# Stores of the gates and of the first Fourier half issued from ScalarE's queue, one tanh later, and another order in the last three iterations of a projection stage

## The chip, the cores and the metric

One core of a Trainium2 chip runs the whole kernel in one launch. The metric is the device time in microseconds (us); several executions are timed and the median counts. One further execution is taken by the hardware profiler. The engines are named as in the profile: PE (TensorE), PEld (its weight loads), DVE (VectorE), ACT (ScalarE), POOL (GpSimd), and SP (SyncE, which does no arithmetic and issues most of the transfers).

## The reference, cut to what matters

Two sequences of 2048 tokens with 1024 features each go through one layer with shared weights:

```python
u = _rmsnorm(h, g_norm)
z = u @ w_in
q, k, v, ga, f, gf = jnp.split(z, ...)
q = _apply_axial_rope(_rmsnorm(q, g_q), cos, sin)
k = _apply_axial_rope(_rmsnorm(k, g_k), cos, sin)
a = _blocked_gqa(q, k, v) * jax.nn.silu(ga)
fo = _fourier_branch(f, w_fmix) * jax.nn.silu(gf)
h = h + jnp.concatenate([a, fo], axis=-1) @ w_out
gate = jax.nn.sigmoid(_rmsnorm(h, g_ple) @ w_ple_gate)
return h + (p @ w_ple) * gate
```

A last RMSNorm follows. `_fourier_branch` is the real part of a 2-D DFT over positions and over the 64 channels of a group, and a linear map of each group. Here the names ga and gf are the columns of the projection that become the gate of the attention and the gate of the Fourier branch.

## The kernel before, in words

**Stages.** The first stage projects (function `project`, in the trace until about 759 us); the second does the attention, the second half of the Fourier branch, the output projection and the rest (until 2596 us). The change lies in the first stage and at the seam between the two.

**Chunks and iterations.** The 4096 tokens are cut into 16 chunks of 256 (two tiles of 128), the first 8 of one sequence and the next 8 of the other. `iteration(i)` (L868 to L927) is written for one chunk, n is 16, and three iterations follow the last chunk to finish it. In each the order of work on every engine is the order of the code: nothing is reordered by a scheduler. An iteration holds, in this order: loads; `square_z`; `lo_q(i-3)` (the second halves of split queries and keys: on DVE the rows named kd, ks, ksum, qs, L796 to L800, on SP the transposes qT and kT); `rope_q(i-2)` (DVE L767, POOL L772); `newton` (an inverse square root in some 20 small DVE steps, from `q_ss` L668 to `q_rs` L686); the matmuls of tile 0 for q, k and v (`mm_tile`); `norm_q` (POOL, qn and t); the folds; and the matmuls of tile 1.

**The sweep.** The other columns of a chunk (f, gf, ga) are a Python generator, the sweep of the chunk, which runs through the next iteration in pieces: `sweep_part(x)` advances it until about x us of matmuls were issued. Its pieces, in order: 24 pairs of matmuls for f (L1056, weights `w_f`, input `uf`; the result is copied by ACT into `ft`, L1024); two gf groups of 24 matmuls of 128x512 (`sweep_f`, through L1072); the first half of the Fourier transform, `first()`, two matmuls on `ft` (L1029) whose result ACT copies into `ge`; and four ga groups of 48 matmuls of 128x256 (`sweep_ga`, rows r = 0 to 3). After each gf and ga group `silu2` does a tanh on ACT (`th`, L1099) and a multiplication on DVE (`gt` or `gat`, L1101; for ga a maximum `tmax` follows, L1089).

**The stores.** Four results go to DRAM and come back in the second stage: `gfd` from `gt` (L1072, two in a chunk), `gd` from `ge` (L1038, one; in a sequence's first chunk two, L1041, and a small `gxd`, L1046), `agd` from `gat` (L1091, four). All are issued from POOL's queue, at the place of the code at which the piece of the sweep stands.

**The folds.** The input `uf` of the f matmuls is made from the chunk's `uc`: POOL adds (f_t L833) and forms sums (f_s L839), ACT rounds the high part (`uf`, L846), and DVE takes the remainder (`uf`, L847). This happens twice per chunk, with one f_s buffer pair: POOL's second f_s waits for DVE's first remainder. POOL's order in an iteration is f_t, f_s, f_t, then the stores that the sweep piece of 12.0 us issued, then the second f_s, then the other stores. ACT's second `uf` stands behind all tanhs of the chunk, and PE's next f group waits for both parts.

**Other work in between.** Every fifth sweep step advances a background generator that prepares the later weights (loads `w_st` on SP L390, conversions `w_o` on ACT L434 and DVE L435, stores wd on SP L437). Every fourth advances `self.ahead`, which takes the maxima of attention's first scores (two matmuls on PE, `a_mx` on DVE L1355).

**A shared ring.** ft, th, gt, ge, gat, w_st, w_o and a few others take turns in one ring of ten buffers (`nw2k = 10`, L181) of 2 KB per partition. A buffer that a store reads is free when the store has landed.

**The end of the stage.** In iterations 16, 17 and 18 `sweep_part(1000.0 if i < n else (6.0, 9.0, 5.0, 100.0)[i - n])` (L905) hands out the rest of the last sweep in portions. The transposes qT and kT of tiles 14 and 15 are issued there, and behind them on SP stands the load `bd` (L1204), for which the Fourier matmuls (L1173) at the head of the second stage wait. The last chunk's gates lie in buffers of their own (`g8`).

Of the kernel before, what the change touches and what calls it, by code (L numbers as in the profile page):

```python
# [48 lines left out]
EVEN = 8 * 33  # L49
# [116 lines left out]
class Build:  # L166
    def __init__(self, ctx, tc, a, y):
        self.ctx, self.tc, self.nc = ctx, tc, tc.nc
        self.a, self.y = a, y
        nc = self.nc  # L170
        ep = ctx.enter_context
        self.const = ep(tc.tile_pool(name="const", bufs=1))
        self.st = ep(tc.tile_pool(name="st", bufs=2))
        self.psF = ep(tc.tile_pool(name="psF", bufs=1, space=PSUM))
        self.psG = ep(tc.tile_pool(name="psG", bufs=2, space=PSUM))
        self.grouped, self.last_stores = False, nc.sync
        self.psX, self.nx = None, 0
        self.dq, self.d1, self.nflush, self.bg = None, [], 0, iter(())
        self.slow, self.passed, self.step = [], set(), 0
        self.ahead = iter(())  # L180
        self.nw2k = 10  # L181
        self.sc = {}
        d = lambda n, s, t: nc.dram_tensor(n, s, t, kind="Internal").ap()
        self.qTd = [d(f"qTd{s}", (NT, 128, 8, 128), F16) for s in range(2)]
        self.kTd = [d(f"kTd{s}", (2, 128, NT // 2, 3, 128), F16) for s in range(2)]
        self.vd = [d(f"vd{s}", (2, 128, NT, 64), F32) for s in range(2)]
        self.gd = [d(f"gd{s}", (128, NT // 2, 512), F32) for s in range(2)]
        self.gxd = [d(f"gxd{s}", (64, EVEN), F32) for s in range(2)]
        self.gfd = [d(f"gfd{s}", (NT, 128, 512), F32) for s in range(2)]
        self.fod = [d(f"fod{s}", (NT, 128, 512), F32) for s in range(2)]  # L190
        self.agd = [d(f"agd{s}", (2, 512, SEQ), F32) for s in range(2)]
        self.bdd = d("bdd", (128, 2, 512), F32)
        self.wd = {}
# [426 lines left out]
    def project(self, P, PU, W, early, later, wkv, wq, wf, wgf, wga, bg, mid):  # L620
# [3 lines left out]
        nc, st = self.nc, self.st  # L624
# [3 lines left out]
        n = len(steps)  # L628
# [239 lines left out]
        def iteration(i):  # L868
            nonlocal stores, stores_next
            if ok(i - 1) and i > 2:  # L870
                VL.pop((i - 1, 1))()
            if i == n + 3:
                self.last_stores = nc.gpsimd
            if ok(i + 4):
                load_x(i + 4, 0)
            if ok(i - 1):
                load_rope(i - 1)
            stores, stores_next = stores_next, []
            for f in stores:
                f()  # L880
            del stores[:]
            sq = square_z(i - 1) if ok(i - 1) else None
            if ok(i - 3):
                lo_q(i - 3)
            if ok(i - 2):
                rope_q(i - 2)
            rs = None
            if ok(i - 1) or ok(i + 2):
                rs = newton(i - 1 if ok(i - 1) else None, i + 2 if ok(i + 2) else None, sq)
            if ok(i):  # L890
                mm_tile(i, 0)
            if ok(i):
                sweep_part(4.0)
                VL.pop((i, 0))()
                sweep_part(4.0)
            if ok(i - 1):
                norm_q(i - 1, rs)
            if folds(i):
                fold_u(i, 0)
                fold_s(i, 0)  # L900
                fold_u(i, 1)
                sweep_part(12.0)
                fold_hl(i, 0)
                fold_s(i, 1)
            sweep_part(1000.0 if i < n else (6.0, 9.0, 5.0, 100.0)[i - n])  # L905
            if folds(i):
                fold_hl(i, 1)
            if ok(i + 2):
                hi_u(i + 2)
                for tt in range(CH):  # L910
                    lo_u(i + 2, tt)
            if ok(i + 4):
                load_x(i + 4, 1)
            if ok(i - 2):
                hi_q(i - 2)
            if ok(i):
                mm_tile(i, 1)
                append(i)
            if ok(i + 3):
                sq_u(i + 3)  # L920
            if i == n - 3:
                early()
            if i == n:
                later()
            if i == n + 3:
                self.drain(bg)
                self.drain(self.ahead)  # L927
# [86 lines left out]
    def sweep_f(self, s, c, uc, UF, i, pool, W):  # L1014

        nc = self.nc
        CH = 2
        w2k = lambda n, k=512: pool.tile([128, 512], F32, name=n, tag="w2k", bufs=self.nw2k)
        F = []
        half = (slice(0, EVEN), slice(EVEN, 512))  # L1020

        def out(ps):
            F.append(w2k("ft"))
            nc.scalar.activation(F[-1][:], ps[:], AF.Copy, scale=self.sc["inv_f"][:])  # L1024

        def first():
            pf = self.bank()
            if c:
                nc.tensor.matmul(pf[:], self.dft1[:], F[0][:], start=True, stop=True)  # L1029
            else:  # L1030
                for y, sl in enumerate(half):
                    for t in range(CH):
                        nc.tensor.matmul(pf[64 * t:64 * t + 64, sl], self.dft1x[:, 2 * t + y], F[t][:, sl],
                                         start=True, stop=True)
            ge = w2k("ge")
            nc.scalar.activation(ge[:], pf[:], AF.Copy)
            if c:
                nc.gpsimd.dma_start(self.gd[s][:, c, :], ge[:])  # L1038
                return 0.86
            for t in range(CH):  # L1040
                nc.gpsimd.dma_start(self.gd[s].rearrange("(g y i) t d -> y g i t d", g=8, y=2)[t, :, :, 0, :],  # L1041
                                    ge[64 * t:64 * t + 64])
            px, gx = self.bank(), w2k("ge")
            nc.tensor.matmul(px[0:64, :EVEN], self.dft1x[:, 4], F[0][:, :EVEN], start=True, stop=True)
            nc.scalar.activation(gx[0:64, :EVEN], px[0:64, :EVEN], AF.Copy)
            nc.gpsimd.dma_start(self.gxd[s], gx[0:64, :EVEN])  # L1046
            return 1.3

        if c:
            ps = self.bank()  # L1050
            uf = UF.pop(i)
            n = 0
            for k in range(8):
                for ia, ib in SPLIT3:
                    for y, sl in enumerate(half):
                        nc.tensor.matmul(ps[:, sl], uf[:, y, ia, k, :], W["f"][:, ib, k, sl], start=n == y == 0,  # L1056
                                         stop=n == 23, skip_group_check=True)
                    n += 1
                yield 0.64
            out(ps)  # L1060
        else:
            for tt in range(CH):
                ps = self.bank()
                yield from self.mm(ps[:], lambda b, k: uc[:, tt, b, k, :], lambda b, k: W["f"][:, b, k, :])
                out(ps)
        for tt in range(CH):
            t = c * CH + tt
            ps = self.bank()
            yield from self.mm(ps[:], lambda b, k: uc[:, tt, b, k, :], lambda b, k: W["gf"][:, b, k, :])
            gt = w2k("gt")  # L1070
            self.silu2(gt[:], ps[:], self.sc["h_gf"], w2k("th"),
                       lambda t=t, gt=gt: nc.gpsimd.dma_start(self.gfd[s][t], gt[:]))  # L1072
        yield first()

    def sweep_ga(self, s, c, uc, pool, W):

        nc = self.nc
# [4 lines left out]
        for r in range(4):  # L1082
            ps = self.bank()
            yield from self.mm(ps[:, :n], lambda b, k: W["ga"][:, b, k, r * 128:(r + 1) * 128],
                               lambda b, k: uc[:, :, b, k, :], n)
            gt, th = (w2k("gat")[:, :n], w2k("th")) if g8 is None else (g8[:, 2 * r], g8[:, 2 * r + 1])

            def more(r=r, gt=gt):
                nc.vector.tensor_reduce(out=self.tmax[s][:, c * 4 + r:c * 4 + r + 1], in_=gt, op=ALU.max,  # L1089
                                        axis=AX.X, apply_absolute_value=True)  # L1090
                nc.gpsimd.dma_start(self.agd[s][1, r * 128:(r + 1) * 128, c * n:(c + 1) * n], gt)  # L1091

            self.silu2(gt, ps[:, :n], self.sc["h_ga"], th, more)

    def silu2(self, out, z, half, th, then):

        nc = self.nc
        n = out.shape[-1]
        nc.scalar.activation(th[:, :n], z, AF.Tanh, scale=half[:])  # L1099

        self.defer(lambda: nc.vector.scalar_tensor_tensor(out=out, in0=th[:, :n], scalar=1.0, in1=z,  # L1101
                                                          op0=ALU.add, op1=ALU.mult), True)
# [941 lines left out]
```

## Time and profile before

| | us |
|---|---|
| median of three executions | 2601.84 |
| the three executions | 2595.85, 2603.52, 2601.84 |
| the profiled execution's own time | 2597.87 |
| its span, first to last instruction | 2595.8 |
| PE busy in the span | 2511.0 |
| POOL busy | 1896.6 |
| DVE busy | 1668.4 |
| ACT busy | 1183.6 |

The 2.1 us between the profiled execution's time and its span lie before the first and behind the last instruction. In the timeline a row gives start and duration of a run of like instructions, engine, line, operation, output<-input, count, and in brackets the engine's idle time before it with what ended that. A row of SP is marked SPq: the engine issues a transfer there, and the duration is that of the issue.

### The profile page before, as it was taken

How to read it: one execution, taken by the hardware profiler on the slowest of the kernel's cores; microseconds unless marked ns; L12 is line 12 of the kernel's file. 1: busy time of each engine (PE TensorE's matmuls, PEld its weight loads, DVE VectorE, ACT ScalarE, POOL GpSimd, SP SyncE). 2: the span in 40 equal slices, each digit the busy share in tenths (PEclk: the TensorE clock that was granted, in tenths of full speed). 3: DMA queues.
4: the chain of work that ended last, by engine and by line, in shares of the span. 5: the costliest groups of instructions: out<-in, count | busy, mean ns of one | idle time of the engine just before them, and what ended most of it. 6: DMA issues, size and time to landing. Idle time of an engine off the chain costs nothing. (4 is left out here: it accounts for less than half of the span.)

```text
span 2595.8 us, 49879 instructions
## 1 busy us (share of the span) xinstructions
PE 2511.0 (97%) x19896; PEld 1384.0 (53%) x19896; DVE 1668.4 (64%) x2382; ACT 1183.6 (46%) x1983; POOL 1896.6 (73%) x1646
## 2 busy tenths in 40 slices
PE   6999989999999999999999999999999999999988
PEld 3566656666656545545545555445544554545533
DVE  7766576777566856566666666666666665766534
ACT  4433353434235545554544545444544444445522
POOL 0465545475659978888888888878887988888840
PEclk9999999999999999999999999999999999999999
DMA  8467588787377742223222233422223322233232
GB/s 259 101 175 198 162 223 230 185 195 180 103 197 248 212 118 62 58 76 78 59 69 75 71 81 88 90 69 63 73 73 82 72 75 63 66 82 76 78 76 53
DMA packets 450265, 297.92 MB, mean 115 GB/s; under 512 B 294000, under 2 KB 394480, under 8 KB 450032
## 3 DMA queue, kind: packets, MB, share of 16 engines
q1 hardware_dynamic: 437952, 256.28, 38.9%
q0 software_dynamic: 12080, 38.46, 4.2%
q8 instruction: 155, 2.54, 0.4%
q14 instruction: 78, 0.64, 0.1%
HBM read 146.12 MB, written 82.45 MB: 88 GB/s over the span
## 5 line engine op out<-in xcount | busy, mean ns | idle before, releaser
L1325 POOL TENSOR_TENSOR acc<-acc,p 128x1024 f32<-128x1024 f32 x384 | 927.6, 2416 | 109.5 <-ACT p L1320 84.6
L1320 ACT ACTIVATE p<-ps_s,s_scale 128x512 f32<-128x512 f32 x1024 | 648.1, 684 | 636.4 <-PE ps_s L1317 613.9
L1355 DVE TENSOR_REDUCE a_mx<-ps_m 128x1 f32<-128x1024 f32 x498 | 608.9, 1223 | 512.0 <-PE ps_m L1347 501.0
L1649 PE MATMUL ps_g<-w_pg,hT 64*128 64x512 f16 x2784 | 494.1, 376 | 3.8 <-DVE seen L1610 2.4
L1383 PE MATMUL ps_o<-p,v 128*64 128x256 f32 x4096 | 468.2, 381 | 0.0
L1317 PE MATMUL ps_s<-q,k 64*128 64x512 f16 x3072 | 433.1, 378 | 1.4 <-ACT p L1320 1.0
L1383 PEld LDWEIGHTS ps_o<-p,v 128*64 128x64 f32 x4096 | 283.7, 137 | 160.4 <-issue 28.5
L504 PEld LDWEIGHTS <-uc 128*128 128x128 f16 x2400 | 236.3, 99 | 231.2 <-DMA uc<-hl 19.5
L1649 PEld LDWEIGHTS <-hT 64*128 64x128 f16 x2784 | 204.8, 94 | 156.9 <-issue 15.7
L1649 PE MATMUL ps_g<-w_wo,mh 64*128 64x512 f16 x1440 | 260.5, 376 | 3.2 <-DVE mh L1554 1.9
L1649 PE MATMUL ps_g<-w_wo,mT 64*128 64x512 f16 x1440 | 257.3, 376 | 0.0
L1317 PEld LDWEIGHTS <-k 64*128 64x128 f16 x3072 | 152.6, 94 | 195.3 <-issue 77.0
L1347 PE MATMUL ps_m<-k,q 64*128 64x512 f16 x996 | 200.8, 377 | 10.2 <-DVE a_mx L1355 9.8
L504 PEld LDWEIGHTS <-w_ga 128*128 128x128 f16 x1536 | 148.8, 98 | 33.5 <-issue 11.9
L1323 POOL TENSOR_TENSOR acc<-p,p 128x1024 f32<-128x1024 f32 x64 | 150.8, 2357 | 11.7 <-ACT p L1320 10.7
L1649 PEld LDWEIGHTS <-mh 64*128 64x128 f16 x1440 | 101.5, 94 | 91.5 <-issue 16.6
L1649 PEld LDWEIGHTS <-mT 64*128 64x128 f16 x1440 | 107.0, 94 | 76.3 <-issue 4.8
L772 POOL TENSOR_TENSOR t<-t,t 128x640 f32<-128x640 f32 x32 | 49.2, 1556 | 121.2 <-DVE t L767 121.2
L1406 DVE RECIPROCAL ps_f<-ps_f 128x256 f32<-128x256 f32 x61 | 107.1, 1756 | 13.6 <-PE ps_f L1399 13.6
L504 PE MATMUL ps_x<-uc,w_ga 128*128 128x256 f16 x1008 | 113.5, 273 | 2.0 <-DVE a_mx L1355 1.4
L504 PE MATMUL ps_x<-w_gf,uc 128*128 128x512 f16 x480 | 108.0, 384 | 2.4 <-DVE a_mx L1355 2.4
L1390 ACT ACTIVATE at<-ps_o,a_scale 128x256 f32<-128x256 f32 x64 | 30.4, 474 | 168.2 <-PE ps_o L1383 168.2
(347 smaller groups left out, 3415.6 us busy)
## 6 DMA issues: line engine op xcount, KB each, us to landing
q<-qTd SPq DMA_DIRECT2D x256, 64.0 KB, 2.2
ag<-agd SPq DMA_DIRECT2D x64, 256.0 KB, 3.5
out<-h POOLq DMA_DIRECT2D x31, 512.0 KB, 3.1
x<-in_x_prompt SPq DMA_DIRECT2D x16, 512.0 KB, 4.9
gfd<-gt POOLq DMA_DIRECT2D x32, 256.0 KB, 2.7
agd<-gat POOLq DMA_DIRECT2D x64, 128.0 KB, 2.8
w_st<-in_w_out SPq DMA_DIRECT2D x32, 256.0 KB, 4.0
w_st<-in_w_ple_gate SPq DMA_DIRECT2D x32, 256.0 KB, 4.0
```

Of the source, the lines that this page charges most:

```text
L504: self.nc.tensor.matmul(ps, lhs(ia, k), rhs(ib, k), start=(i == 0), stop=(i == 3 * ks - 1))
L772: nc.gpsimd.tensor_tensor(out=t1[:, tt], in0=t1[:, tt], in1=t2[:, tt], op=ALU.add)
L1317: nc.tensor.matmul(S[u][e][:], w[sl], q[sl].rearrange("p h q -> p (h q)"), start=j == i == 0, stop=i + 1 == len(todo), skip_group_check=True)
L1320: nc.scalar.activation(p[:, e, :], S[u][e][:], AF.Exp, scale=self.sc["s_scale"][:])
L1323: nc.gpsimd.tensor_tensor(out=ACC[u][:], in0=P[u, 0][:], in1=p[:], op=ALU.add)
L1325: nc.gpsimd.tensor_tensor(out=ACC[u][:], in0=ACC[u][:], in1=p[:], op=ALU.add)
L1347: nc.tensor.matmul(ps[c], Q[u][0][sl, h, :], kt[s, kv, half][sl, :, 0, :], start=True, stop=True)
L1355: nc.vector.reduce_max(MX[u][:, h, half, c:c + 1], x, axis=AX.X)
L1383: nc.tensor.matmul(o[64 * f:64 * f + 64], vt[s, kv, c // 8][:, c % 8, :], p[:, e, f], start=(c == 0), stop=(c == 15))
L1390: nc.scalar.activation(at[:].rearrange("p c q -> p (c q)"), o, AF.Copy, scale=self.sc["a_scale"][:])
L1406: nc.vector.reciprocal(r, r)
L1649: nc.tensor.matmul(g[0][:], g[1](ia, k)[sl], g[2](ib, k)[sl], start=a, stop=z, skip_group_check=True)
```

## The change: what it does

1. The stores gfd, gd, gxd and agd are no longer issued where their results are made. They are put in a list (`self.stores`), and `store_gates()` issues the list's content from ACT's queue. It is called right behind each tanh, and behind the copy `ft`. A result is made by DVE after its tanh, so its store stands behind the next tanh (or the next `ft`).
2. The last chunk's four agd stores (from `g8`) stay on POOL.
3. In iteration 16 a `sweep_part(7.2)` is put ahead of `newton`, in iteration 17 a `sweep_part(3.9)` ahead of `lo_q`, and the table of the portions becomes (3.3, 3.3, 7.0, 100.0).

```diff
+            if i == n + 1:
+                sweep_part(3.9)
             if ok(i - 3):
                 lo_q(i - 3)
             if ok(i - 2):
                 rope_q(i - 2)
             rs = None
+            if i == n:
+                sweep_part(7.2)
             if ok(i - 1) or ok(i + 2):
                 rs = newton(i - 1 if ok(i - 1) else None, i + 2 if ok(i + 2) else None, sq)
...
-            sweep_part(1000.0 if i < n else (6.0, 9.0, 5.0, 100.0)[i - n])
+            sweep_part(1000.0 if i < n else (3.3, 3.3, 7.0, 100.0)[i - n])
...
         def out(ps):
             F.append(w2k("ft"))
             nc.scalar.activation(F[-1][:], ps[:], AF.Copy, scale=self.sc["inv_f"][:])
+            self.store_gates()
...
-                nc.gpsimd.dma_start(self.gd[s][:, c, :], ge[:])
+                self.stores.append((self.gd[s][:, c, :], ge[:]))
...
-                       lambda t=t, gt=gt: nc.gpsimd.dma_start(self.gfd[s][t], gt[:]))
+                       lambda t=t, gt=gt: self.stores.append((self.gfd[s][t], gt[:])))
...
-                nc.gpsimd.dma_start(self.agd[s][1, r * 128:(r + 1) * 128, c * n:(c + 1) * n], gt)
+                d = self.agd[s][1, r * 128:(r + 1) * 128, c * n:(c + 1) * n]
+                if g8 is None:
+                    self.stores.append((d, gt))
+                else:
+                    nc.gpsimd.dma_start(d, gt)
...
+    def store_gates(self):
+        for d, x in self.stores:
+            self.nc.scalar.dma_start(d, x)
+        del self.stores[:]
...
         nc.scalar.activation(th[:, :n], z, AF.Tanh, scale=half[:])
+        self.store_gates()
```

The order of PE's instructions and of SP's is the same before and after. Three places show what moves on the others.

ACT, in the middle of the first stage, from a chunk's second gf tanh (h_gf) to its second `uf`; first before:

```order
L1099 ACTIVATE th<-ps_x,h_gf 128x512
L1036 ACTIVATE ge<-ps_x 128x512
L434 ACTIVATE w_o<-w_st,wf_s 128x512
L1099 ACTIVATE th<-ps_g,h_ga 128x256
L434 ACTIVATE w_o<-w_st,wf_s 128x512 x2
L846 ACTIVATE uf<-f_s 128x2x512
L1099 ACTIVATE th<-ps_g,h_ga 128x256
L434 ACTIVATE w_o<-w_st,wf_s 128x512 x2
L1099 ACTIVATE th<-ps_f,h_ga 128x256
L434 ACTIVATE w_o<-w_st,wf_s 128x512
L1099 ACTIVATE th<-ps_x,h_ga 128x256
L846 ACTIVATE uf<-f_s 128x2x512
```

and the first rows of the same stretch after the change:

```order
L1114 ACTIVATE th<-ps_x,h_gf 128x512
L1107 DMA gfd<-gt 128x512
L1042 ACTIVATE ge<-ps_x 128x512
L435 ACTIVATE w_o<-w_st,wf_s 128x512
L1114 ACTIVATE th<-ps_g,h_ga 128x256
L1107 DMA gfd<-gt 128x512
L1107 DMA gd<-ge 128x512
L435 ACTIVATE w_o<-w_st,wf_s 128x512 x2
L847 ACTIVATE uf<-f_s 128x2x512
L1114 ACTIVATE th<-ps_g,h_ga 128x256
L1107 DMA agd<-gat 128x256
L435 ACTIVATE w_o<-w_st,wf_s 128x512 x2
```

Each tanh is now followed by the store of the result before it: two more agd stores stand in the cut-off rest, one behind each of the two tanhs there, and the fourth agd of a chunk stands behind the next chunk's `ft`.

POOL, the folds of one chunk in the same stage, before:

```order
L833 TENSOR_TENSOR f_t<-uc 128x512 x2
L839 TENSOR_TENSOR f_s<-f_t 128x512 x2
L833 TENSOR_TENSOR f_t<-uc 128x512 x2
L1072 DMA gfd<-gt 128x512 x2
L1038 DMA gd<-ge 128x512
L1091 DMA agd<-gat 128x256
L839 TENSOR_TENSOR f_s<-f_t 128x512 x2
L1091 DMA agd<-gat 128x256 x3
```

After the change the four rows of stores are gone from here, and the four rows of folds stand behind one another.

DVE, at the seam, from the last step of `newton` of tile 15 (q_rs) to the start of the last `lo_q` (the second kd row; t is the rotation of tile 15, and a number in a name only tells buffers apart); first before:

```order
L686 TENSOR_SCALAR q_rs<-rsq_z_8406,inv_kv 128x2x2
L1355 TENSOR_REDUCE a_mx<-ps_x 128x1 x2
L796 TENSOR_TENSOR kd<-kd,ks 128x256
L797 CAST ks<-kd 128x2x2x64
L798 TENSOR_TENSOR kd<-kd,ks 128x256
L799 TENSOR_TENSOR ksum<-t_8062,kd 128x256
L800 TENSOR_TENSOR qs<-t_8062,qs 128x16x64
L767 TENSOR_TENSOR t_8528<-qn,rt 128x16x16 x4
L767 TENSOR_TENSOR t_8528<-qn,rt 128x4x16 x4
L1355 TENSOR_REDUCE a_mx<-ps_x 128x1 x2
L1101 SCALAR_TENSOR_TENSOR gt<-th,ps_x 128x512 x2
L796 TENSOR_TENSOR kd<-kd,ks 128x256
```

and after the change:

```order
L687 TENSOR_SCALAR q_rs<-rsq_z_8480,inv_kv 128x2x2
L1117 SCALAR_TENSOR_TENSOR gt<-th,ps_x 128x512 x2
L797 TENSOR_TENSOR kd<-kd,ks 128x256
L798 CAST ks<-kd 128x2x2x64
L799 TENSOR_TENSOR kd<-kd,ks 128x256
L800 TENSOR_TENSOR ksum<-t_8062,kd 128x256
L801 TENSOR_TENSOR qs<-t_8062,qs 128x16x64
L768 TENSOR_TENSOR t_8586<-qn,rt 128x16x16 x4
L768 TENSOR_TENSOR t_8586<-qn,rt 128x4x16 x4
L1117 SCALAR_TENSOR_TENSOR gat_8599<-gat_8599,ps_x 128x256
L1095 TENSOR_REDUCE tmax_88<-gat_8599 128x1
L797 TENSOR_TENSOR kd<-kd,ks 128x256
```

The two pairs of maxima a_mx are gone from here: all four now stand ahead of `newton`. The two gf products gt stood behind the rotation of tile 15 and now stand ahead of the `lo_q` of tile 14. The first ga product and its maximum stood behind the last `lo_q` and now stand ahead of it.

More of the change, by code (lines that the diff above doesn't have):

```diff
@@ L181, in __init__ @@
         self.nw2k = 10
+        self.stores = []
         self.sc = {}
@@ L1037, in first @@
             if c:
-                nc.gpsimd.dma_start(self.gd[s][:, c, :], ge[:])
+                self.stores.append((self.gd[s][:, c, :], ge[:]))
                 return 0.86
             for t in range(CH):
-                nc.gpsimd.dma_start(self.gd[s].rearrange("(g y i) t d -> y g i t d", g=8, y=2)[t, :, :, 0, :],
-                                    ge[64 * t:64 * t + 64])
+                self.stores.append((self.gd[s].rearrange("(g y i) t d -> y g i t d", g=8, y=2)[t, :, :, 0, :],
+                                    ge[64 * t:64 * t + 64]))
             px, gx = self.bank(), w2k("ge")
@@ L1045, in first @@
             nc.scalar.activation(gx[0:64, :EVEN], px[0:64, :EVEN], AF.Copy)
-            nc.gpsimd.dma_start(self.gxd[s], gx[0:64, :EVEN])
+            self.stores.append((self.gxd[s], gx[0:64, :EVEN]))
             return 1.3
```

## The prediction

> **What bounds the kernel now.** I read the busy row first, then the releasers of PE's waits in the first stage, then PE's clock by stretches.
>
> ```profile
> span 2595.8 us, 49879 instructions
> PE 2511.0 (97%) x19896; PEld 1384.0 (53%) x19896; DVE 1668.4 (64%) x2382; ACT 1183.6 (46%) x1983; POOL 1896.6 (73%) x1646
> ```
>
> PE works 2511.0 of 2595.8 us. The change doesn't touch PE's order, so it can only return what PE loses waiting, 84.8 us in all, and in the part of the program that it edits. PE's waits between 90 and 760 us name that part (total, times, longest):
>
> ```profile
> PE ps_g L1056 <- ACT uf L846: 5.1, 2, 3.6
> PE ps_x L504 <- DVE a_mx L1355: 3.8, 2, 2.4
> PE ps_x L1056 <- ACT uf L846: 2.1, 2, 1.5
> PE ps_x L1056 <- DVE uf L847: 1.9, 2, 1.1
> PE ps_g L1056 <- DVE uf L847: 1.3, 2, 0.7
> ```
>
> The four uf rows sum to 10.4 us: f groups that wait for the fold's result, four chunks in all. The a_mx row, 3.8 us, is the seam. The next view says what the clock adds (columns: stretch, its length, busy time with count of PE, PEld, DVE, ACT, POOL, granted clock, DMA share, GB/s):
>
> ```profile
> 325.00:390.00 65.00, 58.51 (x379) 38.30 (x377) 47.00 (x85) 35.57 (x61) 30.21 (x31) 0.95 0.83 224
> 455.00:520.00 65.00, 65.00 (x443) 43.36 (x442) 47.55 (x123) 30.80 (x59) 31.43 (x36) 1.00 0.77 186
> ```
>
> Where PE waits, the granted clock is 0.95; where it doesn't, PE is busy for all 65 us at 1.00, and there the change can give nothing. Now PE at the four chunks, which I call C, D, E and F:
>
> ```profile
> 153.79 0.61 PE L1056 MATMUL ps_x<-w_f,uf 128*128 128x264 f16 x4 [0.63 <-ACT uf L846]
> 155.49 2.36 PE L1056 MATMUL ps_x<-w_f,uf 128*128 128x264 f16 x20 [1.09 <-DVE uf L847]
> ...
> 284.34 0.61 PE L1056 MATMUL ps_g<-w_f,uf 128*128 128x264 f16 x4 [1.50 <-ACT uf L846]
> 285.60 3.89 PE L1056 MATMUL ps_g<-w_f,uf 128*128 128x264 f16 x20 [0.65 <-DVE uf L847]
> ...
> 330.88 0.61 PE L1056 MATMUL ps_x<-w_f,uf 128*128 128x264 f16 x4 [1.46 <-ACT uf L846]
> 332.27 3.64 PE L1056 MATMUL ps_x<-w_f,uf 128*128 128x264 f16 x20 [0.79 <-DVE uf L847]
> ...
> 379.82 0.61 PE L1056 MATMUL ps_g<-w_f,uf 128*128 128x264 f16 x4 [3.60 <-ACT uf L846]
> 381.08 3.94 PE L1056 MATMUL ps_g<-w_f,uf 128*128 128x264 f16 x20 [0.65 <-DVE uf L847]
> ```
>
> The same twenty matmuls take 2.36 us at C, and 3.89, 3.64 and 3.94 behind the longer waits: 1.53, 1.28 and 1.58 us more. So each longer wait costs its idle time and about 1.5 us of slower matmuls. At stake: C 0.63+1.09 = 1.7, D 1.50+0.65+1.53 = 3.7, E 1.46+0.79+1.28 = 3.5, F 3.60+0.65+1.58 = 5.8; together 14.7 us.
>
> The Trainium skill ("TensorE: Matmul & The Clock Gate", "What's actually happening") puts the half clock down to at least one idle window of about 3.4 us. By that D and E would not have been slowed and would return 2.2 us each; the rows show 1.3 to 1.5 us of slowing behind idle times of 2.2 us in two pieces, and the sum goes by the rows.
>
> **The change part by part: the stores.** Does a store make uf late? F shows it most plainly (POOL, SP and ACT by time):
>
> ```profile
> 362.29 1.11 POOL L1072 DMA_DIRECT2D gfd<-gt  x2
> ...
> 372.06 2.94 POOL L839 TENSOR_TENSOR f_s<-f_t 128x512 f32<-128x512 f32 x2 [7.59 <-DVE uf L847]
> ...
> 364.68 0.34 SPq L390 DMA_DIRECT2D w_st<-in_w_out  x1
> 365.11 0.53 SPq L437 DMA_DIRECT2D wd_wp<-w_o  x1
> ...
> 368.98 0.72 ACT L434 ACTIVATE w_o<-w_st,wf_s 128x512 f16<-128x512 f32 x1 [4.17 <-DMA w_st<-in_w_out]
> ...
> 378.34 0.47 ACT L1099 ACTIVATE th<-ps_x,h_ga 128x256 f32<-128x256 f32 x1 [2.88 <-DMA agd<-gat]
> 378.71 1.05 ACT L846 ACTIVATE uf<-f_s 128x1024 f16<-128x1024 f32 x1
> ```
>
> It is a ring of causes. POOL issues the two gfd behind three fold steps, at 362.29. A w_st load wants a buffer of the shared ring, and SP's queue stands until 364.68. ACT's w_o waits 4.17 us for a load, and ACT's first uf stands behind it, so POOL's second f_s waits 7.59 us. At last ACT waits 2.88 us for an agd store before the tanh ahead of the second uf, and PE waits 3.60 for that uf. After the change no store stands on POOL between folds, and none waits for a fold. I take F at 5.0 of 5.8 (bounds 0 and 5.8), since a store still stands one tanh late. At C both waits (1.7) have the same source and I take them whole; the lower bound is 0. D has a direct cause:
>
> ```profile
> 271.29 0.74 POOL L1072 DMA_DIRECT2D gfd<-gt  x1
> 272.05 0.54 POOL L1038 DMA_DIRECT2D gd<-ge  x1
> 272.58 0.54 POOL L1091 DMA_DIRECT2D agd<-gat  x1
> 280.72 2.48 POOL L839 TENSOR_TENSOR f_s<-f_t 128x512 f32<-128x512 f32 x2 [7.60 <-issue]
> ```
>
> Three stores, 0.74+0.54+0.54 = 1.8 us, stand ahead of the f_s that ends last. Without them uf is 1.8 us sooner: the wait of 1.50 closes, 0.3 of the 0.65 stays, and the slow matmuls go: 3.4. The 7.60 us of POOL's own issue stay. E I take at 2.3, between 0 and 3.5, nearer to the upper end because F, with the same conversions in its chunk, is its nearest row.
>
> **The price on ACT.** Seven issues a chunk. SP's rows above bound one between 0.34 and 0.53 us, POOL's at 0.54; I take 0.5, so 3.5 us a chunk, or 4 to 5 in the stretch of 65 us in which ACT is busy 35.57. ACT's spare time there, 29 us, hides it; without that cover the tanh behind it, and then the uf, would be late by 0.5 a store. ACT also waits at each store for DVE's product, made from the previous tanh; it is long done by the next one, which follows a matmul group later (2.7 us or more). Ahead of the second uf stands one store, 0.5, which F's reserve covers.
>
> **The seam.** The order of PE, DVE, POOL and SP there:
>
> ```profile
> 731.52 5.34 PE L504 MATMUL ps_x<-w_gf,uc 128*128 128x512 f16 x24
> 739.28 7.03 PE L504 MATMUL ps_x<-w_gf,uc 128*128 128x512 f16 x24 [2.42 <-DVE a_mx L1355]
> 748.52 5.40 PE L504 MATMUL ps_x<-uc,w_ga 128*128 128x256 f16 x48 [1.36 <-DVE a_mx L1355]
> 765.46 1.10 PE L1173 MATMUL ps_g<-bd,fT 128*128 128x256 f32 x4 [2.16 <-DMA bd<-bdd]
> ...
> 738.54 1.28 DVE L1355 TENSOR_REDUCE a_mx<-ps_x 128x1 f32<-128x512 f32 x2
> 739.74 0.51 DVE L796 TENSOR_TENSOR kd<-kd,ks 128x256 f32<-128x256 f32 x1
> 745.65 2.22 DVE L767 TENSOR_TENSOR t<-qn,rt 128x256 f32<-128x256 f32 x8
> 748.99 1.27 DVE L1101 SCALAR_TENSOR_TENSOR gt<-th,ps_x 128x512 f32<-128x512 f32 x2
> 752.80 0.42 DVE L796 TENSOR_TENSOR kd<-kd,ks 128x256 f32<-128x256 f32 x1 [2.54 <-ACT ks L786]
> ...
> 748.03 3.04 POOL L772 TENSOR_TENSOR t<-t,t 128x640 f32<-128x640 f32 x2 [1.99 <-DVE t L767]
> ...
> 755.70 2.61 SPq L804 DMA_TRANSPOSE qT<-qs  x2
> 760.37 1.31 SPq L1204 DMA_DIRECT2D bd<-bdd  x1
> ```
>
> With the four a_mx ahead of newton PE's second gf group starts at 736.86 and takes 5.34, not 7.03: it is done at 742.2 instead of 746.3, and with the 1.36 PE reaches attention 5.5 us sooner. But the Fourier matmuls of 765.46 wait for bd, whose load stands on SP behind the transposes, which stand behind the last lo_q, POOL's t, DVE's rotation and tile 14's lo_q, at 739.74. That lo_q now stands behind both gt, and the second needs the tanh of the gf group done at 742.2. With 0.7 of tanh and 0.64 of gt the lo_q begins at 743.5, 3.8 us later. (The four a_mx, 2.56 by 1.28 for two, also push newton, which ended at 738.54, to 741.1; that is ahead of 743.5 and adds nothing.) Some returns: a_mx and gt no longer stand behind the rotation, and the lo_q that took 5.9 us (739.74 to 745.65) took under 2.9 the second time (752.80 to 755.70). So bd comes 0.65 (of a gat and its maximum ahead of the last lo_q) to 3.8 us later; I take +2.5. Then PE's sooner start turns into a longer wait for bd. The other end, with bd no bound, is −5.5.
>
> **Sum.** C 1.7 + D 3.4 + E 2.3 + F 5.0 = 12.4 us less, seam 2.5 more: −9.9. From the profiled execution's own 2597.87 that gives 2588.0. It lies 4.0 under the median of the runs, 2601.84, and these spread from 2595.85 to 2603.52, so for the median I forecast 2590.
>
> **Rivals.**
> - *The seam gains too.* If the transposes wait for less than I think, PE keeps the 5.5: 2597.87 − 12.4 − 5.5 = 2580. For it: the lo_q's 5.9 against 2.9 us. Against: PE already waited 2.16 for bd.
> - *The change doesn't do what it says.* Each store stands a tanh later, the fourth agd of a chunk even behind the next ft, so buffers of the ring come free no sooner and w_st, th and uf wait as before: gaps stay, seam +2.5, 2600. For it: ACT already waits at a tanh for agd (2.88). Against: F's store waited for a fold, and D's stores were direct work of POOL.
> - *Slower: ACT stalls at a store.* The transposes hold SP's issue 1.3 us each (2.61 for two). If a store on ACT cannot be issued meanwhile, the second uf behind it comes 1.3+0.5 = 1.8 us late, in up to 14 chunks. It decides where uf has less than 1.8 us to spare; at four chunks it had none. With half the chunks hit, no gap closed and the seam's +2.5: 2597.87 + 7 × 1.8 + 2.5 = 2613. For it: the second uf stands straight behind a store. Against: beside F's stores SP issues plain transfers of 0.34 and 0.53. The Trainium skill ("Perfetto Trace Analysis", "DMA Instruction — HWDGE") says that transfers of this kind lock one shared descriptor generator for the time of their issue, which is this mechanism; no run here shows it yet, as only SP issued so.
>
> **How the numbers follow.** Chances: forecast 0.50 (its own range 2582 to 2597, from E and F at their bounds), seam gains too 0.15, stores don't help 0.25, ACT stalls 0.10. Two in ten outside: the range is 2578 to 2603, which leaves out the stall and the tails. A measurement tells about 0.3% from no change, 7.8 us, so faster means below 2594: four fifths of the forecast and all of the seam's gain, 0.55; slower is the stall, 0.10; same is the rest, 0.35.
>
> **What would show it.** Right: no uf waits of PE at C, D and F and a clock of 1.00 from 260 to 390; POOL's second f_s straight behind its f_t; no releaser gfd on SP's loads; PE's wait for bd grown to some 8 us or more, with the first attention scores sooner. Wrong: uf waits of the same size with agd still named ahead of the tanh; SP's or ACT's issues far above 0.54 us; the bd load no later than 760.37 less what was gained before it.

## The result, and the profile after

| | before | after |
|---|---|---|
| median, us | 2601.62 | 2586.09 |
| lowest to highest (4 executions each) | 2595.85 to 2603.52 | 2585.38 to 2587.85 |
| the profiled execution, us | 2597.87 | 2585.38 |
| its span, us | 2595.8 | 2583.6 |

The ratio is 0.9945 (95% interval 0.9933 to 0.9957): 15.5 us less in the median. The median before in this table has one execution more than the one that the forecast started from.

First PE's waits between 90 and 760 us in the changed kernel (total, times, longest; the line numbers are those of the changed kernel, 1 to 16 higher), all six of them:

```profile
PE ps_g L1189 <- DMA bd<-bdd: 5.8, 1, 5.8
PE ps_g L1243 <- DVE gat L1117: 3.4, 1, 3.4
PE ps_x L505 <- DMA uc<-hl: 1.2, 1, 1.2
PE ps_f L505 <- DVE inv_ga L311: 1.1, 1, 1.1
PE ps_x L505 <- DVE w_mxs L397: 0.6, 1, 0.6
PE ps_x L1035 <- ACT ft L1029: 0.2, 1, 0.2
```

No row with uf is left, nor the a_mx row. At the seam two waits stand in its place, for bd and for a ga product (gat). The two stretches in which PE had waited are full now, at clock 1.00; the second is the one that had 58.51 and 0.95:

```profile
260.00:325.00 65.00, 65.00 (x451) 44.08 (x450) 41.27 (x78) 32.07 (x54) 26.45 (x22) 1.00 0.68 191
325.00:390.00 65.00, 65.00 (x445) 43.71 (x444) 45.10 (x92) 29.08 (x50) 34.27 (x30) 1.00 0.88 247
```

What SP's loads of w_st waited for between 90 and 760 us (total, times, longest) has this row for gfd in the kernel before:

```profile
SPq L390 <- DMA gfd<-gt: 33.7, 6, 12.5
```

and this one in the changed kernel, 6.8 us instead of 33.7 (shorter, but not gone):

```profile
SPq L391 <- DMA gfd<-gt: 6.8, 5, 2.2
```

What a store costs ACT, the view of its line says (count, then shortest/median/longest in ns, then the first and last start; the two gxd are left out here):

```profile
L1107 ACTq DMA_DIRECT2D agd<-gat x60: 321/326/568, 99.9 to 716.2; - x60
L1107 ACTq DMA_DIRECT2D gfd<-gt x32: 326/326/390, 82.6 to 730.1; - x32
L1107 ACTq DMA_DIRECT2D gd<-ge x18: 327/445/1359, 92.5 to 730.5; - x18
```

**Where the time went.** PE's order is the same in both, so the start of the same instruction can be compared. The two matmuls of the first Fourier half (on ft) stand once in each chunk. The table gives the start of the first of them in the profiled execution of a kernel less that of before; the column heads are their starts in the kernel before, and the chunks C to F end ahead of the second, fourth, fifth and sixth column. The last column is the first Fourier matmul behind bd. e1 to g2 are the kernels of the experiments below.

| kernel | 122.6 | 168.0 (C) | 253.1 | 299.7 (D) | 346.5 (E) | 395.2 (F) | 658.8 | 704.9 | 765.5 (bd) |
|---|---|---|---|---|---|---|---|---|---|
| after | +1.1 | −0.9 | −0.9 | −5.0 | −9.2 | −15.4 | −15.4 | −15.6 | −14.2 |
| e1, stores only | +1.2 | −0.9 | −0.9 | −5.0 | −9.2 | −15.4 | −15.4 | −15.5 | −15.7 |
| e2, tail only | +0.7 | +0.9 | +0.9 | −2.6 | −0.9 | −0.7 | −0.7 | +1.1 | +3.2 |
| e3, POOL behind the folds | +0.7 | −0.3 | −0.3 | −4.3 | −1.4 | −4.8 | −3.7 | +2.4 | +1.8 |
| e5, ACT at once | +4.6 | +2.5 | +2.5 | −1.5 | −5.8 | −9.8 | −7.6 | −1.8 | −0.5 |
| f1, gfd and gd | +1.3 | −1.6 | −1.6 | −5.7 | −9.9 | −16.1 | −16.1 | −16.2 | −17.4 |
| f2, agd | −1.8 | −4.7 | −4.7 | −8.7 | −7.3 | −6.6 | −4.8 | +1.4 | +0.9 |
| g2, gt apart | +0.2 | +2.2 | +2.2 | −1.8 | −2.1 | −5.6 | +5.3 | +10.2 | +10.3 |

In the changed kernel C gave 2.1 us, D 4.0, E 4.3 and F 6.2, 16.5 together; 1.3 were lost between the last chunk and bd. Beside that, 1.1 were lost before C and 2.0 in the second stage, where neither PE's order nor any store is edited. That stage differs by as much between executions: in the profiled one of e1 it was 4.8 us shorter than before. So totals are compared by medians only, and single executions place by place.

### The profile page after: what moved, and what is told of

The parts are those of the page before. It is cut to its first block, busy times and chain, and to the rows that moved or that the text cites. A ratio compares the mean times of both kernels' runs of the same rounds, so it can differ in the third digit from the quotient of the medians.

```text
span 2583.6 us, 49739 instructions
## 1 busy us (share of the span) xinstructions
PE 2503.1 (97%) x19896; PEld 1381.7 (53%) x19896; DVE 1655.9 (64%) x2382; ACT 1185.5 (46%) x1983; POOL 1834.5 (71%) x1534
## 5 line engine op out<-in xcount | busy, mean ns | idle before, releaser
L1363 PE MATMUL ps_m<-k,q 64*128 64x512 f16 x996 | 200.7, 377 | 15.5 <-DVE a_mx L1371 15.3
L505 PEld LDWEIGHTS <-w_ga 128*128 128x128 f16 x1536 | 148.8, 98 | 33.2 <-issue 10.4
L1339 POOL TENSOR_TENSOR acc<-p,p 128x1024 f32<-128x1024 f32 x64 | 151.0, 2359 | 13.0 <-ACT p L1336 12.2
L840 POOL TENSOR_TENSOR f_s<-f_t 128x512 f32<-128x512 f32 x56 | 71.8, 1303 | 53.9 <-DVE uf L848 41.5
```

Of the source, the lines that this page charges most:

```text
L505: self.nc.tensor.matmul(ps, lhs(ia, k), rhs(ib, k), start=(i == 0), stop=(i == 3 * ks - 1))
L840: nc.gpsimd.tensor_tensor(out=FS[h][:, y], in0=x[:, 0], in1=x[:, 1], op=op)
L1339: nc.gpsimd.tensor_tensor(out=ACC[u][:], in0=P[u, 0][:], in1=p[:], op=ALU.add)
L1363: nc.tensor.matmul(ps[c], Q[u][0][sl, h, :], kt[s, kv, half][sl, :, 0, :], start=True, stop=True)
```

## The experiments

Each was timed in five rounds beside the kernel before, on the same chip as the others of its group. Medians, and the ratio to before with its 95% interval:

| | median, us | ratio |
|---|---|---|
| e1, stores only | 2584.81 | 0.9940 (0.9927 to 0.9954) |
| e2, tail only | 2602.63 | 1.0009 (0.9998 to 1.0019) |
| e3, stores on POOL behind the folds | 2604.24 | 1.0016 (1.0005 to 1.0027) |
| e5, stores on ACT at once | 2599.41 | 0.9998 (0.9987 to 1.0008) |
| f1, gfd and gd on ACT | 2581.80, again 2584.47 | 0.9930 (0.9917 to 0.9943), 0.9931 (0.9916 to 0.9945) |
| f2, agd on ACT | 2601.60 | 1.0005 (0.9992 to 1.0018) |
| b2, second gt late | 2584.57 | 0.9938 (0.9926 to 0.9951) |
| b1, bd on ACT | 2583.57 | 0.9938 (0.9925 to 0.9950) |
| g2, gt in buffers of its own | 2608.61 | 1.0030 (1.0018 to 1.0041) |
| the changed kernel again | 2585.33 | 0.9943 (0.9930 to 0.9956) |
| h1, f1 with the new tail and bd on ACT | 2586.58 | 0.9943 (0.9931 to 0.9956) |

### The stores, or the tail (e1, e2)

e1 takes the new tail out of the changed kernel; e2 puts it into the kernel before.

```diff
-            if i == n + 1:
-                sweep_part(3.9)
...
-            if i == n:
-                sweep_part(7.2)
...
-            sweep_part(1000.0 if i < n else (3.3, 3.3, 7.0, 100.0)[i - n])
+            sweep_part(1000.0 if i < n else (6.0, 9.0, 5.0, 100.0)[i - n])
```

> Only the stores move to ACT's queue (one tanh later); the last iterations are as before. Theory (the stores alone closed the four uf waits, and the new tail gave back what it gained): no uf wait of PE over 0.3 us at C, D, E, F; at the seam the a_mx waits (3.8 us) return but the Fourier matmuls resume at 765.46 - 15.5 = about 750; time 2584 us, so the same as the changed kernel or 1 to 2 us under it. Rival (the tail carries a good part of the gain): 2592 or more, with the Fourier matmuls after 755.

> Only the last iterations are changed; the stores stay on POOL. Theory: the uf waits of about 10 us and their slow matmuls stay, the a_mx waits at the seam go, the wait for bd grows to some 6 us, net +1 us: 2600 to 2603 us, no change from before. Rival (the tail carries a good part): 2592 or less, with the Fourier matmuls sooner than 760.

The stores alone give the whole gain, 2584.81; the tail alone gives nothing that can be told from no change, 2602.63. In e1's table row the chunks move as in the changed kernel to 0.1 us. PE's waits at the seam by releaser, in e1:

```profile
PE ps_x L505 <- DVE a_mx L1367: 5.4, 2, 3.0
PE ps_g L1239 <- DMA g_in<-gd: 2.0, 1, 2.0
PE ps_g L1185 <- DMA bd<-bdd: 0.4, 1, 0.4
```

and the two places in e2, from PE's timeline:

```profile
759.22 1.65 PE L1231 MATMUL ps_g<-c,g_in 128*128 128x128 f32 x6 [3.51 <-DVE gat L1105]
768.68 1.97 PE L1177 MATMUL ps_g<-bd,fT 128*128 128x256 f32 x4 [3.85 <-DMA bd<-bdd]
```

With the old tail PE waits 5.4 us for maxima and hardly for bd; with the new one it doesn't wait for the gf groups but 3.5 for a ga product and 3.9 for bd. The wait changes its name and the Fourier matmuls don't start sooner: in e2 they lost 2.1 us from the column before (+1.1 to +3.2), in the changed kernel 1.3, in e1 they won 0.2.

### Which stores (f1, f2)

```diff
 # f1: agd stays where it was, on POOL
-                if g8 is None:
-                    self.stores.append((d, gt))
-                else:
-                    nc.gpsimd.dma_start(d, gt)
+                nc.gpsimd.dma_start(d, gt)
```

f2 is the reverse: the lines of gfd, gd and gxd are those of before, agd goes through the list. Both have the old tail.

> The stores gfd, gd and gxd go from ACT's queue, agd stays on POOL at its old place; the tail is as before. Theory (gfd and gd are what stands ahead of the second f_s on POOL and what loads of w_st wait for): most of the gain, 2586 to 2592 us, uf waits of PE under 4 us. Rival (ACT's waits for agd ahead of the second uf, 2.9 to 8.0 us, are the cause): uf waits of 6 us and more stay, 2596 us or more.

> The other half: agd goes from ACT's queue, gfd, gd and gxd stay on POOL at their old place; the tail is as before. Theory: uf waits of 6 us or more stay, loads of w_st wait for gfd some 30 us in sum, 2595 to 2601 us. Rival: 2590 us or less.

f1 has the whole gain; f2's median is that of the kernel before. Since f1's median was the lowest, it was run once more beside the changed kernel:

> Only gfd, gd and gxd from ACT's queue, agd on POOL, tail as before, once more beside the changed kernel. If leaving agd on POOL and the old tail is the better kernel: 3 to 5 us under the changed kernel of the same call. If the two only differed by chance: within 2 us of it.

> The changed kernel once more, beside the others on one chip: 2584 to 2587 us, ratio 0.9935 to 0.995.

Side by side the two differed by 0.9 us (2584.47 and 2585.33), with intervals that overlap: no better kernel is shown. What holds f2 back is in the row of SP's loads

```profile
SPq L391 <- DMA gfd<-gt: 37.7, 6, 11.2
```

and in PE's timeline at E and F:

```profile
324.13 0.77 PE L1058 MATMUL ps_x<-w_f,uf 128*128 128x264 f16 x4 [3.41 <-ACT uf L847]
325.53 3.48 PE L1058 MATMUL ps_x<-w_f,uf 128*128 128x264 f16 x20 [0.63 <-DVE uf L848]
...
371.58 0.61 PE L1058 MATMUL ps_g<-w_f,uf 128*128 128x264 f16 x4 [2.65 <-ACT uf L847]
373.14 4.45 PE L1058 MATMUL ps_g<-w_f,uf 128*128 128x264 f16 x20 [0.96 <-DVE uf L848]
```

With gfd on POOL SP's loads wait 37.7 us for it, as before, and E and F stay. C and D did close in f2's profiled execution (2.9 and 4.0 us in the table), but it lost that again by the end of the stage. The rival that ACT's waits for agd are the cause falls: 60 agd stores moved, and the median is no lower.

### The queue, or the moment (e3, e5)

e3 is e1 with the list issued from POOL's queue, and the stores that stood between the folds behind the second f_s:

```diff
                 fold_u(i, 1)
+                self.hold = True
                 sweep_part(12.0)
                 fold_hl(i, 0)
                 fold_s(i, 1)
+                self.hold = False
+                self.store_gates()
...
     def store_gates(self):
         for d, x in self.stores:
-            self.nc.scalar.dma_start(d, x)
+            self.nc.gpsimd.dma_start(d, x)
...
         nc.scalar.activation(th[:, :n], z, AF.Tanh, scale=half[:])
-        self.store_gates()
+        if not self.hold:
+            self.store_gates()
```

e5 is the kernel before with the stores on ACT's queue, each where its result is made and not one tanh later:

```diff
-                       lambda t=t, gt=gt: nc.gpsimd.dma_start(self.gfd[s][t], gt[:]))
+                       lambda t=t, gt=gt: nc.scalar.dma_start(self.gfd[s][t], gt[:]))
 # the same for gd and gxd, and for agd but in the last chunk
```

> The stores stay on POOL, but those of a chunk that would stand between its folds are issued behind the second f_s; the tail is as before. It parts two ways in which stores and folds hold each other. If the stores held the folds (POOL's time): D closes and most of C, E and F too, time 2588 or less. If the folds held the stores, and these the ring of buffers (my theory for C, E and F): the stores come later still, D's wait shrinks, the waits of C, E and F stay or grow, loads of w_st wait for gfd 30 us or more in sum: 2596 to 2610 us.

> The stores stand on ACT's queue at the place where their results are made, not one tanh later, so ACT waits at each for DVE's product; the tail is as before. If the delay by a tanh matters (ACT stalls at stores, tanh and uf late): ACT's waits at stores sum to 100 us or more in the stage, uf waits of PE return, 2590 us or more. If ACT has time enough: ACT waits about 1 us at a store, no uf waits, 2583 to 2586 us, the same as with the stores one tanh later.

e3 is no gain: at 2604.24 its whole interval lies just above 1. It parts the four chunks: C, D and F shrink, E grows, −1.4 from −4.3. (D alone proves little, since it closed in e2 too, where no store was moved.) That speaks for some of the delay being POOL's time ahead of the second f_s, and for the stores' lateness coming back elsewhere. Neither of the two answers that I had written down came out pure: the time is the second's, but SP's loads of w_st waited 10.2 us for gfd and not 30 or more.

e5 closes most of the four waits too (−9.8 at F; 3.6 us of uf waits are left of 10.4) and loses it again by the end of the stage. Its time is in the range of the first answer. One place where it lost time (ACT of e5 in order of time):

```profile
651.79 0.34 ACTq L1072 DMA_DIRECT2D gfd<-gt  x1
652.24 0.69 ACT L1100 ACTIVATE th<-ps_x,h_gf 128x512 f32<-128x512 f32 x1 [6.74 <-DMA kTd<-kT]
653.68 0.33 ACTq L1072 DMA_DIRECT2D gfd<-gt  x1
654.13 0.60 ACT L1036 ACTIVATE ge<-ps_x 128x512 f32<-128x512 f32 x1 [1.20 <-DVE gt L1102]
656.97 0.33 ACTq L1038 DMA_DIRECT2D gd<-ge  x1
660.59 0.47 ACT L1100 ACTIVATE th<-ps_g,h_ga 128x256 f32<-128x256 f32 x1 [5.86 <-DMA bdd<-bd]
```

The first gfd store is issued at 651.79, though DVE had its product at 646.2, and ACT's next tanh, behind it, has waited 6.74 us with a transfer of SP's as releaser. Most of that is no loss: in the kernel before the same tanh waits 5.87 us for its matmuls, so the store added 0.9. The gd store goes at 656.97, 2.2 us after ge was done. In this trace's records the transfers of SP's and of ACT's queue signal their landing on the same eight semaphores (counters), and a store is issued right behind the landing of the transfer that had its semaphore before: the first gfd store behind SP's qTd, landed at 651.72, the gd store behind SP's transpose qT, landed at 656.89. That these are the waits is read from the records; it wasn't tried apart. The tanh at 660.59 comes 5.3 us behind its matmuls, which end at 655.24. Up to 657.30 it stands behind the gd store, and for the other 3.3 us it waits for a buffer of the ring that the store of bdd reads. That second wait isn't due to a store on ACT: at the same place in e3 the tanh waits 6.93 us with bdd as releaser, and in the kernel before 2.45 for its matmuls. The late tanhs pass on: DVE's products and the maxima behind them are late, and PE waits for a_mx (PE of e5):

```profile
662.62 0.37 PE L1348 MATMUL ps_x<-k,q 64*128 64x512 f16 x1 [0.96 <-DVE a_mx L1356]
666.95 0.37 PE L1348 MATMUL ps_x<-k,q 64*128 64x512 f16 x1 [0.95 <-DVE a_mx L1356]
668.93 7.03 PE L504 MATMUL ps_x<-wr_q,uc 128*128 128x512 f16 x24 [1.01 <-DVE a_mx L1356]
```

That stretch costs e5 5.8 us (−7.6 to −1.8). e3 and f2, whose tanhs are late at the same place too, lose 6.1 and 6.2 there; e1, f1 and the changed kernel 0.2 at most. So the distance of a tanh matters: e5 and e1 differ only in where on ACT's queue a store stands. That the queue matters as well e3 shows less cleanly, since its stores also stand at another place. How much of e5's loss is the stores' waits and how much the late bdd stays open.

### The ring (g2)

```diff
-            gt = w2k("gt")
+            gt = pool.tile([128, 512], F32, name="gt", tag="gtown", bufs=2)
...
-        self.nw2k = 10
+        self.nw2k = 8
```

> The kernel before, stores on POOL at their old places, but gt has two buffers of its own and the shared ring has eight instead of ten, so no load, tanh or conversion waits for a buffer that a gfd store still reads. Theory (the ring carries the delay: what matters is that loads of w_st wait for late gfd stores): SP's loads no longer name gfd, the uf waits of E and F shrink to under 2 us in sum, D's stays, 2588 to 2593 us. Rival (POOL's time and order ahead of the second f_s is the cause, the ring only follows): uf waits of 6 us and more stay, 2597 us or more.

2608.61, slower, with 12.6 us of uf waits: by these numbers the rival's answer, and not the theory's. But the places have changed. PE's timeline of g2 at C, at a chunk that had no wait before, and at F:

```profile
156.06 4.02 PE L1056 MATMUL ps_x<-w_f,uf 128*128 128x264 f16 x20 [2.35 <-DVE uf L847]
...
471.39 1.03 PE L1056 MATMUL ps_f<-w_f,uf 128*128 128x264 f16 x4 [3.69 <-ACT uf L846]
...
375.80 0.61 PE L1056 MATMUL ps_g<-w_f,uf 128*128 128x264 f16 x4 [1.63 <-ACT uf L846]
377.06 2.36 PE L1056 MATMUL ps_g<-w_f,uf 128*128 128x264 f16 x20 [0.65 <-DVE uf L847]
```

F's waits fell from 4.25 to 2.28 us and its slow matmuls went; E kept 2.0 us of waits, C's grew, and new ones came. What SP's loads wait for now is gd:

```profile
SPq L390 <- DMA gd<-ge: 16.9, 4, 9.6
```

No gfd row is left, but the ring of eight is short. The experiment changed two things and can't settle the ring's share. A longer ring with nothing else changed wasn't tried, so how much of the delay goes by the ring and how much by POOL's time stays open.

### The seam (b2, b1, h1)

b2 is the changed kernel with the portion of iteration 17 behind `rope_q` again, so that the second gt no longer stands ahead of tile 14's `lo_q`. b1 is the changed kernel with

```diff
-        nc.sync.dma_start(self.bd[:], self.bdd)
+        nc.scalar.dma_start(self.bd[:], self.bdd)
```

and h1 is f1 with the new tail and that line.

> The changed kernel, with the sweep portion of iteration 17 behind lo_q and the rotation again, so only the second gt moves back behind the rotation of tile 15 on DVE; the a_mx stay early. Theory (the second gt ahead of tile 14's lo_q is what passes the seam's gain on into the wait for bd): that lo_q begins 3.6 us sooner, bd's load and the Fourier matmuls 2.5 to 3.6 us sooner, 2583 us. Rival (bd is late for another reason, as POOL's order or the transposes): the wait for bd stays at 5 us or more, 2586 us.

> The changed kernel, with the one load of bd issued from ACT's queue (behind two exponentials, some 5 us sooner) and no longer behind the transposes on SP's. Theory (SP's order alone makes bd late): the wait of 5.8 us for bd falls under 1 us, the Fourier matmuls start at 746 instead of 751, 2581 us. Rival (the next wait, for gf_in or g_in or the maxima, takes its place): the wait moves to another releaser and the time stays at 2585 to 2586 us.

> gfd, gd and gxd from ACT's queue, agd on POOL, the new tail, and the load of bd from ACT's queue. If the seam can return something once bd doesn't stand behind the transposes: Fourier matmuls at 745 to 746, 2578 to 2581 us. If the next wait (g_in) takes its place as it did with bd alone: a g_in wait of 4 us or more, 2581 to 2584 us.

b2 brought nothing that can be told from the changed kernel (2584.57), and my theory of it falls. DVE's first and last rows of that `lo_q` in the changed kernel:

```profile
727.86 1.51 DVE L797 TENSOR_TENSOR kd<-kd,ks 128x256 f32<-128x256 f32 x1
730.67 1.22 DVE L801 TENSOR_TENSOR qs<-t,qs 128x1024 f16<-128x1024 f32 x1
```

the same in b2:

```profile
726.97 1.11 DVE L797 TENSOR_TENSOR kd<-kd,ks 128x256 f32<-128x256 f32 x1
731.28 2.29 DVE L801 TENSOR_TENSOR qs<-t,qs 128x1024 f16<-128x1024 f32 x1
```

and POOL beside it in b2:

```profile
729.16 4.72 POOL L756 TENSOR_TENSOR t<-qn,rt 128x512 f32<-128x512 f32 x4
```

Started right behind `newton`, the `lo_q` runs beside POOL's t and takes 6.6 us (726.97 to 731.28+2.29); where it starts a gt later, with POOL nearly done, it takes 4.0 (727.86 to 730.67+1.22). Most of the sooner start is eaten by the slower run.

In b1 bd's load leaves ACT at 739.87 instead of SP at 746.06, PE's wait for bd is gone, and the next one has its place (PE of b1):

```profile
754.85 1.62 PE L1243 MATMUL ps_g<-c,g_in 128*128 128x128 f32 x6 [4.56 <-DMA g_in<-gd]
```

In h1 that wait is 5.43.

b1's median is 2583.57, h1's 2586.58; neither is told apart from the changed kernel, and no version beat it beyond doubt. That load of g_in stands on SP behind the same transposes as bd did.

## Why the prediction was right, step by step

- **The bound.** Right: between C and the seam the changed kernel's row of the table moves only at C, D, E and F, and there by the waits and the slow matmuls behind them.
- **The stores.** Right in mechanism, too small in size: 16.5 us instead of 12.4. C gave 2.1 (taken 1.7), D 4.0 (3.4), E 4.3 (2.3), F 6.2 (5.0). The rows put 14.7 at stake, of which I took 12.4: I held 1.2 us of E and 0.8 of F back for a store that still stands late, and 0.3 of D; nothing stayed. The other 1.8 us the rows don't show as idle or slow. A row of PE's timeline that is followed without a wait runs 0.17 us into the next one (at C 155.49+2.36 against 157.68), so each wait costs 0.17 more than its idle time says, 0.34 in a chunk with two: C gave 2.1 for 1.7 of idle time with no slow matmul. And at E alone the slow clock ran on past the twenty matmuls: the 48 of gf behind them took 10.80 us to the next row (335.70 to 346.50), and 10.36 in the changed kernel. Four times 0.34 and these 0.44 make the 1.8. The granted clock in the kernel before, at C, D, E and F:

```profile
150.40:157.60 7.20, 5.48 (x50) 4.44 (x48) 4.73 (x6) 5.29 (x8) 1.72 (x4) 1.00 0.45 168
285.40:288.70 3.30, 3.10 (x15) 2.23 (x16) 2.54 (x3) 3.30 (x8) 0.00 (x0) 0.50 0.31 78
333.20:336.50 3.30, 3.30 (x16) 2.06 (x14) 2.54 (x6) 3.27 (x9) 0.00 (x0) 0.50 0.59 116
381.00:384.30 3.30, 3.22 (x16) 2.29 (x17) 2.47 (x4) 3.30 (x8) 0.00 (x0) 0.50 0.24 48
```

The Trainium skill ("TensorE: Matmul & The Clock Gate", "What's actually happening") puts the half clock down to at least one idle window of about 3.4 us. D and E had the clock of 0.50 behind idle times of 2.15 and 2.25 us in two pieces, so for them the Trainium skill and the rows differ, and the measurement decides.
- **D's margin.** The step that only three stores of 1.8 us stand ahead of the f_s was wrong, with the right sign. In the changed kernel POOL's f_s starts at 268.60, not 280.72, 12 us sooner: POOL's all-reduce ahead of it also came sooner, at 260.52 instead of 271.01, and so did the chunk's first f_s, at 249.70 instead of 258.57. POOL as a whole ran some 9 us sooner without the stores, and the step counted only the three that stand directly ahead. And in e2, with the stores where they were, D gave 3.5 us by itself and E took 1.7 back, so single rows of D and E move between executions.
- **The price on ACT.** By the medians 0.33 us for gfd and agd, just below the bounds of 0.34 to 0.54, and 0.45 for gd; covered, as PE's waits show.
- **The wait on a store for DVE.** I wrote that DVE is long done one tanh later; e5 shows what happens without that tanh, and that at the place shown a wait on SP's transfers comes in beside it, which the prediction had only as the rival of a stalled ACT.
- **The seam.** Right: the gf groups no longer wait, and the wait for bd grew from 2.16 to 5.82. It cost 1.3 where I took 2.5, between 0.65 and 3.8. (The lower bound was too low: in the kernel before a gat and its maximum take 0.8 us, from 755.55 to 756.34 on DVE.) The row of DVE in the changed kernel that carried the step:

```profile
727.25 0.69 DVE L1117 SCALAR_TENSOR_TENSOR gt<-th,ps_x 128x512 f32<-128x512 f32 x1 [3.00 <-ACT th L1114]
```

The second gt does hold the `lo_q` until 727.86, as the prediction said; the shorter run of that `lo_q`, 4.0 instead of 5.9 us, gives part of it back.
- **The rivals.** That the stores don't help is out (e1). That the seam gains too is out (e1 against the changed kernel, e2). ACT does stand still at stores where the tanh's distance is missing (e5), and there by DVE's product or a transfer's landing. As a stall at the issue it is no rule: 26 gfd and agd stores of the changed kernel were issued while a transpose was in issue on SP, and the longest of these took 0.46 us. Single issues beside a transpose were longer, 1.36 us (gd at 92.5) and 1.69 (gxd at 94.5) in the changed kernel and 2.04 (agd at 566.24) in e1; no uf wait of PE followed in either. The Trainium skill ("Perfetto Trace Analysis", "DMA Instruction — HWDGE") states a lock of one shared descriptor generator. Whether the single long issues are that lock no run here shows.
- **The signs.** Three held: no uf waits, a clock of 1.00 from 260 to 390, and the load of bd at 746.06, 1.3 us later than 760.37 less the 15.6 won before it. Two came out weaker than written: SP's loads still name gfd (6.8 us), and the wait for bd is 5.8 us and not 8, because PE first waits 3.4 for a ga product. POOL's second f_s doesn't follow its f_t at once at D: the all-reduce stands between.
- **Why the number fits.** 2590 was forecast and 2586.09 measured. In the profiled executions the sum was −9.9 against −12.2 of the span: 4.1 more from the stores, 1.2 more from the seam, 1.1 and 2.0 lost before C and in the second stage. That the miss is only 4 us is luck in part: the mis-sized terms and the losses elsewhere have opposite signs. The own range of the forecast, 2582 to 2597, has a lower end that E and F at their bounds don't give; they give 2588, and the measured time lies below that.

## What to carry to other kernels

Look first for what waits for a transfer that is itself waiting in a queue behind computation: here SP's loads stood 33.7 us for gfd, and moving gfd and gd, three of a chunk's seven stores, was worth as much as moving all. When a store goes to a busy engine's queue, put it behind an instruction that is released later than the store's data, or that engine stands still at it (e5). And at a seam where one wait hands over to the next, follow the chain to the instruction that must start sooner before the order ahead of it is changed: e2, b2, b1 and h1 each took one wait away and met another.

## What the runs showed of the hardware that wasn't expected

- In the kernel before the granted clock was 0.50 for the whole of 3.3 us at each of D, E and F, behind idle times of 2.15, 2.25 and 4.25 us: 1.5 to 1.7 us lost each time, however long the wait. The idle time alone doesn't decide it: C with 1.72 us kept 1.00, and so did F in g2 with 2.28 (its row of 2.36 for twenty matmuls), while E in g2 was slowed behind 2.01 (4.02 for the same twenty).
- A gfd or agd store took 0.33 us of the queue when issued from ACT, and 0.54 (agd) to 0.58 (gfd) when issued from POOL, by the medians.
- DVE's kd, ks, ksum and qs steps took 2.8 us with POOL idle, and up to 6.6 beside POOL's tensor operations: what runs beside a step can matter more than when it starts.
